# Two-layer encoder trunk in float32: nine pairs of column blocks a layer take seven block products instead of eight in their first two K chunks

## The chip, the cores and the metric

The kernel runs on one core of a Trainium2 chip, in one launch. The metric is the device time of that execution in microseconds (us), as the median of several runs. TensorE (PE) multiplies, VectorE (DVE) and ScalarE (ACT) work elementwise, GpSimd (POOL) does a few small powers, and the queue of SyncE (SP) issues all the transfers. Each engine works through its own instructions in the order of the program.

## The reference

A trunk of 2 layers on 256 tokens of width 2048, all in float32. Cut to what matters:

```python
for l in range(DEPTH):                              # 2
    h = rmsnorm(x, pre_norm_g[l])
    proj = jnp.einsum('bsd,dn->bsn', h, w_in[l])    # 2048 x 17920: 35 column blocks of 512
    (qa, ka, va, qb, kb, vb, qc, kc, vc, za, zb, zc, gates) = jnp.split(proj, split_points, axis=-1)
    ya = neighbourhood_attention(qa, ka, va, rpb[l])            # 8 heads
    yb = gqa_attention(rope(rmsnorm(qb)), rope(rmsnorm(kb)), vb)  # 8 heads
    yc = dilated_mixture(qc, kc, vc)                            # 12 heads in 3 groups
    ga, gb, gc = jnp.split(sigmoid(gates + b_gate[l]), 3, axis=-1)
    merged = (ga * ((ya * silu(za)) @ w_branch_a[l]) + gb * ((yb * silu(zb)) @ w_branch_b[l])
              + gc * ((yc * silu(zc)) @ w_branch_c[l]))
    out = jnp.einsum('bsd,de->bse', merged, w_out[l])           # 4 column blocks of 512
    x = x + rmsnorm(out, post_norm_g[l])
```

## The kernel before, in words

**A product in three matmuls.** Every float32 operand is split in two halves of type fp32r, high and low (`split`, and `emit_hi` / `emit_lo` for weights): a cast on ACT gives the high half, a subtraction on DVE the low one. `mm3` (L169) multiplies high by high, high by low and low by high into the same accumulator, and leaves out low by low. So one block product (128 of K, 128 tokens, 512 columns) is three matmuls of 128x128 by 128x512.

**Blocks, chunks, halves.** The work is a list of column blocks (`Blk`) of 512 columns: first the projections of the dilated mixer C (one gate block, three of q, three of k, three of v), then those of A (two units of four blocks), then B (five), then four merges (`merge`: three gate blocks, then three branch projections of 8, 4 and 8 K tiles, in the order a, c, b), then four output blocks. A block's K is cut into chunks of 256, that is one transfer of 512 KB (`raw`), one cast (`wh`) and one subtraction (`wl`) of 128x1024. The tokens are two halves T of 128, each with an accumulator (`acc`) of its own. `stream` is the list of all chunks; for each chunk `run_half` issues six matmuls for T = 0 and six for T = 1. In the last block of a layer and the first of the next (`lag`) the second half runs six chunks behind the first.

**How far ahead things are written.** The program writes the instructions of all engines in one loop over (chunk, half). Ahead of each half `ahead` writes the transfers up to 6 chunks, casts up to 3 and subtractions up to 2 chunks ahead of the one that is multiplied (more in `far` blocks). What is written first on an engine is done first there. All tiles of weights and most others come from one pool `up` of 47 tiles of 4 KB a partition; accumulators come from the pool `mm` of 4 banks, with four more banks for scores (`sc`), head outputs (`o`) and transposes (`tp`, two).

**What runs in between.** After the second half of a chunk there is a slot (`slot`, L102). In it the kernel takes two steps of waiting evacuations (`evq`: one of a half block, as a rule), a step of each active job, and starts a job: light ones are the turns of a finished block (`tr_job`: DVE transposes of 32x32, a transfer to DRAM and back, then a split), heavy ones the heads of attention. So the evacuation of a block's first half is written in the slot after its last chunk, that of its second half one slot later. `hold` keeps all evacuations of a layer back until the sum of squares of x is there (`stats`, written after chunk 5 of the second block, `second`).

**The pair that there is already.** The first two output blocks (`mate`, `mated`) are interleaved: six chunks of the one, six of the other, then the last two of each, since the last merged block arrives late.

**Where the change touches.** The list `order` of (chunk, half) is made at the end, before the main loop (L756 to L772). The change makes it where the stream is made.

## Time and profile before

| | us or share |
|---|---|
| median of 3 runs | 2019.52 (2019.33 to 2019.94) |
| profiled execution, its own time | 2019.99 |
| profiled execution, its span | 2017.9 |
| TensorE's share of the chain of waits that ended last | 92% |

The span is from the first to the last instruction of the profiled execution; its own time has some 2.1 us around it. In the groups of instructions an operation is named by its line, engine and tiles, with how many there are, their busy time and the mean of one in ns. Matmuls are pipelined, so the duration of one overlaps with the next; how fast they follow one another is read from their starts. An idle time stands with what ended it: "<-DVE wl L202" is a wait for the subtraction of line 202. HBM was read at 231 GB/s over the span.

### The profile page before, as it was taken

To read this page: it belongs to the slowest core of one execution; us is meant where nothing else is said; L and a number is where in the kernel's file an instruction comes from. 1 tells how busy PE (TensorE), PEld (TensorE's weight loads), DVE (VectorE), ACT (ScalarE), POOL (GpSimd) and SP (SyncE) were. 2 spreads that over 40 slices of the span, in tenths; PEclk is the share of its full clock that TensorE was granted. 3 is DMA by queue.
4 is the path that set the end of the run, shared out by engine and by line. 5 is a ranking of instruction groups with operands and counts; after the bars stand their busy time and mean duration, and the time that the engine had idled before them with its cause. 6 is when DMAs were issued, how large, how long until landed. Compare 5 with 4: busy or idle time off the path is not lost.

```text
span 2017.9 us, 24528 instructions
## 1 busy us (share of the span) xinstructions
PE 2002.0 (99%) x9098; PEld 1660.7 (82%) x9098; DVE 1271.1 (63%) x1565; ACT 995.9 (49%) x1482; POOL 21.5 (1%) x31
## 2 busy tenths in 40 slices
PE   9999999999999999999999999999999999999998
PEld 7888888888788888888888888888887888888886
DVE  6554576768677465645665545767677775646554
ACT  6544465646464444443564444555465644443432
POOL 0000000000000000000000000000000000000000
PEclk9999999999999999999999999999999999999999
DMA  8667467756666756675647664768566666556653
GB/s 330 245 258 269 158 248 258 262 209 239 226 245 236 267 189 227 225 239 213 235 166 266 263 243 146 266 234 301 198 246 234 239 243 246 214 198 233 219 220 124
DMA packets 171720, 468.06 MB, mean 232 GB/s; under 512 B 15440, under 2 KB 58576, under 8 KB 171600
## 3 DMA queue, kind: packets, MB, share of 16 engines
q1 hardware_dynamic: 171600, 466.50, 63.9%
q8 instruction: 71, 1.16, 0.2%
q14 instruction: 49, 0.40, 0.1%
HBM read 427.11 MB, written 39.32 MB: 231 GB/s over the span
## 4 chain that ended last, share of the span: by engine, by line
PE 92%; DVE 3%; ACT 3%; DMA 1%; issue 0%; SPq 0%; DVEq 0%; POOLq 0%; ACTq 0%
PE acc L173 30%; PE acc L174 30%; PE acc L172 30%; ACT wh L197 1%; DVE wl L202 1%; DVE tt L150 1%; ACT sp L373 1%; PE o L174 0%; PE o L173 0%; PE o L172 0%; ACT sp L384 0%; DMA raw<-in_wpack_dram 0%; PE sc L174 0%; PE sc L450 0%; PE o L480 0%
## 5 line engine op out<-in xcount | busy, mean ns | idle before, releaser
L202 DVE TENSOR_TENSOR wl<-raw,wh 128x1024 fp32r<-128x1024 f32 (+1 forms) x706 | 833.7, 1214 | 169.9 <-ACT wh L197 169.7
L173 PE MATMUL acc<-wl,hTh 128*128 128x512 f32 x2240 | 873.6, 390 | 5.1 <-DVE wl L202 5.1
L172 PE MATMUL acc<-wh,hTh 128*128 128x512 f32 x2240 | 875.6, 391 | 0.6 <-ACT wh L197 0.6
L174 PE MATMUL acc<-wh,hTl 128*128 128x512 f32 x2240 | 872.0, 389 | 0.0
L197 ACT CAST wh<-raw 128x1024 fp32r<-128x1024 f32 (+1 forms) x706 | 706.2, 1042 | 268.4 <-DMA raw<-in_wpack_dram 155.3
L173 PEld LDWEIGHTS acc<-wl,hTh 128*128 128x128 f32 x2240 | 420.9, 188 | 94.8 <-DVE wl L202 10.0
L174 PEld LDWEIGHTS acc<-wh,hTl 128*128 128x128 f32 x2240 | 420.5, 188 | 87.7
L172 PEld LDWEIGHTS acc<-wh,hTh 128*128 128x128 f32 x2240 | 420.9, 188 | 87.0 <-ACT wh L197 1.8
L172 PE MATMUL acc<-wh,yTh 128*128 128x512 f32 x320 | 124.5, 389 | 0.0
L173 PE MATMUL acc<-wl,yTh 128*128 128x512 f32 x320 | 124.5, 389 | 0.0
L174 PE MATMUL acc<-wh,yTl 128*128 128x512 f32 x320 | 124.5, 389 | 0.0
L598 ACT ACTIVATE g<-g 128x512 f32<-128x512 f32 x48 | 30.4, 633 | 177.7 <-DVE g L597 177.7
L597 DVE SCALAR_TENSOR_TENSOR g<-acc,rsx,bg 128x512 f32<-128x512 f32 x48 | 35.9, 747 | 127.9 <-PE acc L174 127.8
L172 PE MATMUL acc<-wh,mTh 128*128 128x512 f32 x256 | 100.0, 390 | 0.0
L174 PE MATMUL acc<-wh,mTl 128*128 128x512 f32 x256 | 99.6, 389 | 0.0
L173 PE MATMUL acc<-wl,mTh 128*128 128x512 f32 x256 | 99.6, 389 | 0.0
L373 ACT ACTIVATE sp<-sp,nm 128x256 f32<-128x256 f32 (+1 forms) x48 | 27.6, 577 | 131.4 <-DVE nm L368 131.4
L150 DVE STREAM_TRANSPOSE tt<-tok 128x512 f32<-128x512 f32 (+1 forms) x72 | 73.3, 1057 | 0.0
L609 DVE SCALAR_TENSOR_TENSOR g<-g,acc 128x512 f32<-128x512 f32 x48 | 32.8, 684 | 61.2 <-PE acc L174 61.1
L174 PEld LDWEIGHTS acc<-wh,yTl 128*128 128x128 f32 x320 | 60.1, 188 | 12.5
L172 PEld LDWEIGHTS acc<-wh,yTh 128*128 128x128 f32 x320 | 60.1, 188 | 12.3
L173 PEld LDWEIGHTS acc<-wl,yTh 128*128 128x128 f32 x320 | 60.1, 188 | 12.3
(111 smaller groups left out, 1086.5 us busy)
## 6 DMA issues: line engine op xcount, KB each, us to landing
raw<-in_wpack_dram SPq DMA_DIRECT2D x558, 512.0 KB, 6.5
raw<-in_wo_dram SPq DMA_DIRECT2D x64, 512.0 KB, 7.6
turn<-tt SPq DMA_DIRECT2D x50, 512.0 KB, 3.0
tx<-turn SPq DMA_DIRECT2D x50, 512.0 KB, 5.6
raw<-in_wa_dram SPq DMA_DIRECT2D x32, 512.0 KB, 3.4
raw<-in_wb_dram SPq DMA_DIRECT2D x32, 512.0 KB, 4.6
turn<-tt SPq DMA_DIRECT2D x34, 256.0 KB, 2.2
tx<-turn SPq DMA_DIRECT2D x34, 256.0 KB, 4.3
```

Source lines behind the costliest of these rows:

```text
L150: nc.vector.transpose(out=tt[:, :, T].rearrange("p j (h a) -> p h j a", h=n), in_=srcs[T].rearrange("p (h b j) -> p h j b", h=n, j=4))
L172: nc.tensor.matmul(out_, lhsT=lh, rhs=rh, start=first, stop=False)
L173: nc.tensor.matmul(out_, lhsT=lh, rhs=rl, start=False, stop=False)
L174: nc.tensor.matmul(out_, lhsT=ll, rhs=rh, start=False, stop=last)
L197: nc.scalar.copy(HI[i][:, k], RAW[i][:, k])
L202: nc.vector.tensor_tensor(out=LO[i][:, k], in0=RAW[i][:, k], in1=f32(HI[i][:, k]), op=ALU.subtract)
L373: nc.scalar.activation(p[:, i], sc[:, i], AF.Exp, bias=nm[:, i:i + 1], scale=1.0 if f is None else f[:, i:i + 1], accum_out=sm[:, i:i + 1])
L597: nc.vector.scalar_tensor_tensor(g, ps, S["rs"][T], BG[i], op0=ALU.mult, op1=ALU.add)
L598: nc.scalar.activation(g, g, AF.Tanh, scale=0.5)
L609: nc.vector.scalar_tensor_tensor(G[i][:, T], G[i][:, T], 1.0, ps, op0=ALU.add, op1=ALU.mult)
```

## The change

In a pair of blocks that stand next to each other the first two chunks are taken together. For a chunk of 256 of K, two blocks of 512 columns and 256 tokens, the activations are a 2x2 matrix of blocks (token half by K tile) and the weights one (K tile by column block); their product takes eight block products, and seven by Strassen's method in Winograd's form. The pairs are the eight blocks of mixer C after the first two (four pairs), the first two gate blocks of each merge (four pairs) and the first two output blocks.

- Four combinations of the activations (`combos`) are made for each of the first two chunks of a layer's h and of its merged rows, five DVE operations and a split each. They are written behind the first half of chunks 6 and 7 of the block `second`, and of chunks 1 and 2 of the last merge's last branch projection.
- For each unit (one chunk of both blocks) DVE makes four combinations of the weights in two tiles (`unit_hi`), in the order of the program ahead of the cast of B. A is the first block's chunk as it is, B and C are combinations, D is one of them and is taken for both units in one tile.
- The seven products of both units are summed into seven accumulators, at most six at a time, in the steps s1 to s6 of `two_blocks`; the plain chunk 2 of the two blocks is put between them. Four sums on DVE (`total`) and a copy on ACT bring the products together in two tiles (`keep`), and `whole` adds one of these to each accumulator, in place, ahead of its evacuation.
- Ahead of and in a pair (`near`: from three chunks before it) transfers run 8, casts 6 and subtractions 5 places ahead, at most two of each for one half.
- The pool `mm` has six banks, and transposes take the tags of `sc` and `o`.
- From chunk 3 the chunks of the two blocks alternate; the interleaving of the first two output blocks by sixes is gone.

```diff
+LA_UNIT, NEAR = 5, 4
+UNITS = 2
...
-    mm = ctx.enter_context(tc.tile_pool(name="mm", bufs=4, space=PSUM))
+    mm = ctx.enter_context(tc.tile_pool(name="mm", bufs=6, space=PSUM))
...
-        tp = aux.tile([P, 4, P], F32, name="tp", bufs=2)
+        flow["tp"] += 1
+        tp = aux.tile([P, 4, P], F32, name="tp", tag=("sc", "o")[flow["tp"] % 2])
...
+    def unit_hi(u, what):
+        if what == "B":
+            r1, r2 = RAW[u, "A"], RAW[u, "B"]
+            ta, tb = U("ta", [2, 512]), U("tb", [2, 512])
+            minus(ta[:, 0], r2[:, 0], r1[:, 0])
+            minus(ta[:, 1], r2[:, 1], ta[:, 0])
+            minus(tb[:, 0], r2[:, 1], r2[:, 0])
+            minus(tb[:, 1], r1[:, 1], ta[:, 1])
+            RAW[u, "D"] = RAW.pop((u, "B"))
+            RAW[u, "B"], RAW[u, "C"] = ta, tb
+        if what == "D":
+            u.h["D"] = U("wh", [2, 512], FR)
+            for k, v in enumerate(u.all):
+                nc.scalar.copy(u.h["D"][:, k], RAW[v, "D"][:, 1])
+        else:
+            u.h[what] = U("wh", [2, 512], FR)
+            nc.scalar.copy(u.h[what], RAW[u, what])
...
     def ahead(i):
         n = len(stream)
         b = stream[i][0]
         la, room = (8, 13) if b.far else (0, 6)
+        near = any(isinstance(x[0], Unit) for x in stream[i:i + NEAR])
+        if near:
+            la, room = LA_UNIT, 12
...
-            most = 9 if key == "raw" else flow["split"]
+            most = 9 if key == "raw" else min(flow["split"], 2) if near else flow["split"]
...
+    def product(ps_, units, lhs, what, k, alone):
+        for n, u in enumerate(units):
+            x = units[0] if what == "D" else u
+            h, lo = x.h[what], x.lo[what]
+            q = n if what == "D" else k
+            mm3(ps_, lhs(u), (h[:, q], lo[:, q]), n == 0, alone and n == len(units) - 1)
+
+    def two_blocks(one, two):
...
+        for u in units:
+            stream.extend([(u, "A"), (u, "B")])
+        p1 = len(stream)
+        stream.append((one, UNITS))
+        stream.extend((u, "C") for u in units)
+        d = len(stream)
+        stream.append((head, "D"))
+        rest = len(stream)
+        stream.append((two, UNITS))
+        for kc in range(UNITS + 1, one.nc):
+            stream.extend([(one, kc), (two, kc)])
...
+        def s1():
+            new("p1", "p5")
+            product(bank["p1"], units, plain(0, 0), "A", 0, True)
+            product(bank["p5"], units, comb(0), "B", 0, True)
+            keep["c11"], keep["p16"] = room()
+            nc.scalar.copy(keep["c11"], bank.pop("p1"))
+        def s2():
+            new("a")
+            product(bank["a"], units, plain(1, 0), "A", 1, False)
+        def s3():
+            new("p6")
+            product(bank["p6"], units, comb(1), "B", 1, True)
+            total("p16", bank.pop("p6"), keep["c11"])
...
+        def s4():
+            new("d")
+            product(bank["d"], units, plain(1, 1), "C", 1, False)
+            keep["c12"], keep["c21"] = room()
+            total("c12", bank.pop("p5"), keep["p16"])
+        def s5():
+            new("p7")
+            product(bank["p7"], units, comb(2), "C", 0, True)
...
+        def s6():
+            new("c")
+            product(bank["c"], units, comb(3), "D", 0, False)
...
+            total("c21", bank["p7"], keep["p16"])
+            keep["c22"] = keep.pop("p16")
+            total("c22", bank.pop("p7"), keep["c12"])
+            new("w")
+        def whole(evac, of):
+            def f(T, x):
+                k = keep.pop(of[T])
+                nc.vector.tensor_tensor(out=x, in0=x, in1=k, op=ALU.add)
+                yield from evac(T, x)
+            return f
...
+        order.extend([(p1 - 1, s1), (p1, s2), (p1, 0), (p1, s3), (d - 1, s4), (p1, 1), (d, s5), (d, s6),
+                      (rest, 0), (rest + 1, 0), (rest, 1), (rest + 1, 1)])
+        order.extend((i, T) for i in range(rest + 2, len(stream)) for T in range(2))
...
+        def combos(stat, kc):
+            h, lo, j = stat(2 * kc)
+            t = U("cf", [2, 512])
+            a = t[:, 0].rearrange("p (k n) -> p k n", k=2)
+            c = t[:, 1].rearrange("p (k n) -> p k n", k=4)
+            nc.vector.tensor_tensor(out=a, in0=f32(h[:, j:j + 2]), in1=f32(lo[:, j:j + 2]), op=ALU.add)
+            a11, a21, a12, a22 = (a[:, k, T * P:(T + 1) * P] for k in range(2) for T in range(2))
+            nc.vector.tensor_tensor(out=c[:, 0], in0=a21, in1=a22, op=ALU.add)
+            minus(c[:, 1], c[:, 0], a11)
+            minus(c[:, 2], a11, a21)
+            minus(c[:, 3], a12, c[:, 1])
+            r = U("cs", [2, 4, P], FR)
+            split(c, r[:, 0], r[:, 1])
+            return r
...
+            gs = [proj(23 + 4 * i + nb, evac_g(i), pre=pre(i)) for i in range(3)]
+            gs[0].pair(gs[1])
...
+        for k in (1, 3, 5, 7):
+            cb[k].pair(cb[k + 1])
+        for kc in range(UNITS):
+            second.at("after", (6 + kc, 0), lambda kc=kc: CH.update({kc: combos(stat_h, kc)}))
...
-        outs[0].mate, outs[1].mated = outs[1], True
+        outs[0].pair(outs[1])
+        for kc in range(UNITS):
+            blocks[-5].at("after", (1 + kc, 0), lambda kc=kc: CM.update({kc: combos(stat_m, kc)}))
...
     for i, T in order:
         b, kc = stream[i]
+        if callable(T):
+            ahead(i)
+            T()
+            if T.__name__ in ("s1", "s3", "s5"):
+                slot()
+            continue
```

## Rows read from the trace of the kernel before

**Rows 1.** The page: busy time of each engine, its share, its instructions.

```profile
PE 2002.0 (99%) x9098; PEld 1660.7 (82%) x9098; DVE 1271.1 (63%) x1565; ACT 995.9 (49%) x1482; POOL 21.5 (1%) x31
```

**Rows 2.** Groups of instructions: line, engine, operation, count, busy us, mean ns, idle before.

```profile
L172 PE MATMUL acc<-wh,hTh 128*128 128x512 f32 x2240 | 875.6, 391 | 0.6 <-ACT wh L197 0.6
L202 DVE TENSOR_TENSOR wl<-raw,wh 128x1024 fp32r<-128x1024 f32 x702 | 831.1, 1217 | 169.8 <-ACT wh L197 169.7
L197 ACT CAST wh<-raw 128x1024 fp32r<-128x1024 f32 x702 | 703.9, 1045 | 268.4 <-DMA raw<-in_wpack_dram 155.3 <-DMA raw<-in_wo_dram 44.3 <-PE acc L173 23.7
...
L611 DVE TENSOR_TENSOR g<-g 128x512 f32<-128x512 f32 x32 | 22.1, 691 | 1.1
...
L132 ACT ACTIVATE qkh<-tx 128x512 fp32r<-128x512 f32 x32 | 18.4, 623 | 10.6 <-DMA tx<-turn 10.6
...
L525 DVE TENSOR_TENSOR s<-acc,ropeg 128x128 f32<-128x128 f32 x8 | 1.9, 283 | 0.0
```

**Rows 3.** Waits: who waited for whom, us in total, times, longest.

```profile
PE acc L173 <- DVE wl L202: 5.1, 9, 1.2
```

**Rows 4.** Timeline of TensorE, end of layer 0's last merge: start us, us, instruction.

```profile
916.70 0.39 PE L172 MATMUL acc<-wh,yTh 128*128 128x512 f32 x1
...
919.42 0.39 PE L172 MATMUL acc<-wh,mTh 128*128 128x512 f32 x1
```

**Rows 5.** Timeline of DVE there, idle time before in brackets.

```profile
910.56 0.69 DVE L611 TENSOR_TENSOR g<-g 128x512 f32<-128x512 f32 x1
911.17 3.49 DVE L202 TENSOR_TENSOR wl<-raw,wh 128x1024 fp32r<-128x1024 f32 x3
918.26 0.69 DVE L609 SCALAR_TENSOR_TENSOR g<-g,acc 128x512 f32<-128x512 f32 x1 [3.60 <-PE acc L174]
...
923.18 2.04 DVE L150 STREAM_TRANSPOSE tt<-g 128x512 f32<-128x512 f32 x2
...
934.05 1.29 DVE L134 TENSOR_TENSOR mTl<-tx,mTh 128x512 fp32r<-128x512 f32 x2 [4.32 <-ACT mTh L132]
```

**Rows 6.** Timelines of DVE and ACT, second block of layer 0.

```profile
39.46 1.23 DVE L202 TENSOR_TENSOR wl<-raw,wh 128x1024 fp32r<-128x1024 f32 x1 [1.09 <-ACT wh L197]
...
43.16 0.16 DVE L249 TENSOR_REDUCE v<-ss 128x2 f32<-128x8 f32 x1 [0.15 <-ACT junk L245]
...
44.63 0.15 DVE L256 SCALAR_TENSOR_TENSOR rsx<-rs_y 128x2 f32<-128x2 f32 x1
...
51.04 0.69 ACT L330 ACTIVATE tok<-acc,rsx 128x512 f32<-128x512 f32 x1 [3.07 <-PE acc L174]
```

**Rows 7.** Timelines of DVE and ACT, second block of layer 1.

```profile
1025.08 8.03 DVE L202 TENSOR_TENSOR wl<-raw,wh 128x1024 fp32r<-128x1024 f32 x7
...
1054.04 0.69 ACT L330 ACTIVATE tok<-acc,rsx 128x512 f32<-128x512 f32 x1 [12.22 <-PE acc L174]
```

**Rows 8.** Busy time by stretch, mixer C: us, PE, PEld, DVE, ACT, POOL.

```profile
56.00:99.00 43.00, 43.00 (x191) 35.59 (x191) 23.30 (x22) 20.81 (x27) 0.00 (x0) 1.00 0.70 260
```

**Rows 9.** Busy time of layer 0's first merge, first two blocks; DVE's timeline before.

```profile
540.00:583.50 43.50, 41.68 (x201) 34.26 (x200) 34.19 (x60) 25.85 (x52) 1.01 (x1) 1.00 0.63 218
...
530.57 1.16 DVE L150 STREAM_TRANSPOSE tt<-sp 128x256 f32<-128x256 f32 x2
```

**Rows 10.** Timeline of DVE, end of layer 0's first merge.

```profile
726.21 3.49 DVE L202 TENSOR_TENSOR wl<-raw,wh 128x1024 fp32r<-128x1024 f32 x3
733.30 0.69 DVE L609 SCALAR_TENSOR_TENSOR g<-g,acc 128x512 f32<-128x512 f32 x1 [3.60 <-PE acc L174]
```

**Rows 11.** TensorE at start and end; the column after POOL is its clock.

```profile
1.45 4.45 PE L89 MATMUL acc<-warm 128*128 128x512 bf16 x10 [1.45 <-DVE warm L86]
...
2009.21 0.39 PE L174 MATMUL acc<-wh,mTl 128*128 128x512 f32 x1
...
2012.00:2014.00 2.00, 0.00 (x0) 0.00 (x0) 2.00 (x4) 0.00 (x0) 0.00 (x0) 0.95 0.55 200
2014.00:2016.00 2.00, 0.00 (x0) 0.00 (x0) 0.05 (x1) 0.00 (x0) 0.00 (x0) 0.50 0.98 308
```

More of the change, by code (lines that the diff above doesn't have):

```diff
@@ L39, in __init__, with pair @@
         self.far = False
-        self.mate = None
-        self.mated = False
+        self.twin = None
+        self.twinned = False
         self.before = {}
         self.after = {}
+    def pair(self, other):
+        self.twin, other.twinned = other, True
     def at(self, when, key, f):
         getattr(self, when).setdefault(key, []).append(f)
+class Unit:
+    far = False
+    def __init__(self, one, two, kc):
+        self.one, self.two, self.kc = one, two, kc
+        self.h, self.lo = {}, {}
 @with_exitstack
@@ L92, in trunk @@
     evq, light, heavy, active = deque(), deque(), deque(), []
-    flow = dict(turn=0, cool=0, hold=True, slot=0, split=9)
+    flow = dict(turn=0, tp=0, cool=0, hold=True, slot=0, split=9)
     def later(g, wait=0):
@@ L179, in trunk @@
     RAW, HI, LO = {}, {}, {}
+    order, ps = [], {}
     def emit_raw(i):
         b, kc = stream[i]
+        if isinstance(b, Unit):
+            if kc in "AB":
+                x = (b.one, b.two)[kc == "B"]
+                if b.kc == 0 and x.pre:
+                    x.pre()
+                RAW[b, kc] = U("raw", [2, 512])
+                nc.sync.dma_start(out=RAW[b, kc], in_=x.w[b.kc].rearrange("p (k n) -> p k n", k=2))
+            return
         if kc == 0 and b.pre:
@@ L203, in emit_lo, with minus, unit_lo @@
         del RAW[i]
+    def minus(out_, a, b):
+        nc.vector.tensor_tensor(out=out_, in0=a, in1=b, op=ALU.subtract)
+    def unit_hi(u, what):
[15 more added lines that the diff above has]
+            nc.scalar.copy(u.h[what], RAW[u, what])
+    def unit_lo(u, what):
+        u.lo[what] = U("wl", [2, 512], FR)
+        if what == "D":
+            for k, v in enumerate(u.all):
+                minus(u.lo["D"][:, k], RAW[v, "D"][:, 1], f32(u.h["D"][:, k]))
+                del RAW[v, "D"]
+        else:
+            minus(u.lo[what], RAW[u, what], f32(u.h[what]))
+            del RAW[u, what]
     def ahead(i):
@@ L219, in run_half @@
         b, kc = stream[i]
+        first = 2 * UNITS if b.twinned and T else -1 if b.twin or b.twinned else 0
         wh, wl = HI[i], LO[i]
@@ L615, in evac_p @@
                 return f
-            for i in range(3):
-                proj(23 + 4 * i + nb, evac_g(i), pre=pre(i))
+            gs = [proj(23 + 4 * i + nb, evac_g(i), pre=pre(i)) for i in range(3)]
+            gs[0].pair(gs[1])
             for i, w, nk, ub in ((0, wbr_a, 8, (("a", 0), ("a", 1))), (2, wbr_c, 4, (("c", 0),)),
@@ L723, in trunk @@
         for b in bl:
-            if b.mate:
-                m = b.mate
-                stream += [(b, kc) for kc in range(6)] + [(m, kc) for kc in range(6)]
-                stream += [(c, kc) for c in (b, m) for kc in range(6, 8)]
-            elif not b.mated:
-                stream += [(b, kc) for kc in range(b.nc)]
+            i = len(stream)
+            if b.twin:
+                two_blocks(b, b.twin)
+            elif not b.twinned:
+                stream += [(b, kc) for kc in range(b.nc)]
+                if b.lag:
+                    a = [(i + k, 0) for k in range(b.nc)]
+                    c = [(i + k, 1) for k in range(b.nc)]
+                    order += a[:LAG]
+                    for k in range(b.nc - LAG):
+                        order += [a[LAG + k], c[k]]
+                    order += c[b.nc - LAG:]
+                else:
+                    order += [(i + k, T) for k in range(b.nc) for T in range(2)]
     nc.sync.dma_start(out=gpre, in_=pre_g)
@@ L754, in trunk @@
     st["hi"] = st["lo"] = 7
-    order = []
-    i = 0
-    while i < len(stream):
-        b = stream[i][0]
-        n = b.nc
-        if b.lag:
-            a = [(i + k, 0) for k in range(n)]
-            c = [(i + k, 1) for k in range(n)]
-            order += a[:LAG]
-            for k in range(n - LAG):
-                order += [a[LAG + k], c[k]]
-            order += c[n - LAG:]
-        else:
-            n = 1
-            order += [(i, T) for T in range(2)]
-        i += n
-    ps = {}
     for i, T in order:
         b, kc = stream[i]
+        if callable(T):
[4 more added lines that the diff above has]
+            continue
         for f in b.before.get((kc, T), ()):
```

59 lines of the change are left out of this document (50 added, 9 removed).

## The prediction, made before the change was run

> **What bounds the kernel now.** I read the page first. TensorE is busy 99% of the span, VectorE (DVE) is busy 63%, ScalarE (ACT) 49% [rows 1]. Then the groups of instructions: 2240 × 3 of the matmuls are of one form, and the reader is to see next to them the splitting of the weights, a cast on ACT (1.05 us) and a subtraction on DVE (1.22 us) for each chunk [rows 2]. TensorE waits in all 5.1 us for that subtraction [rows 3]. So time falls only with the number of matmuls, as long as DVE delivers in time. The timeline gives the price of a matmul: a chunk of twelve begins at 916.70 and the next at 919.42, so 2.72 us a chunk and 0.227 us a matmul [rows 4] (the 0.39 us of the groups overlaps with the next matmul).
>
> **What it removes.** A pair's first two chunks were 8 block products of 6 matmuls each; seven are left. That is 6 matmuls a pair, 18 pairs in two layers, 108 × 0.227 = **24.5 us**.
>
> **What it adds on DVE and ACT.** Per pair, by the groups [rows 2]: eight differences of 128x512 (0.69 each [rows 2]; 0.61 from one to the next that doesn't need it, 910.56 to 911.17 [rows 5], so 2.6 for the four of a unit), 5.2 us; seven chunks to split instead of four (two each of A, B and C, and two halves of D), 3 × 1.16 = 3.5 us with the spacing of 3.49 for three [rows 5]; four sums and four additions ahead of the evacuations, 8 × 0.69 = 5.5 us. Together 14 us of DVE a pair, 18 × 14 = 252 us, so DVE goes to some 76%. ACT gets 3 casts and a copy, 3.8 us a pair. Four times (two chunks, two stages) a layer the combinations of the activations come on top: one 0.69, four of 128x128 at 0.28, a cast of 0.62 on ACT that DVE waits for, a subtraction of 0.69, with two hand-overs 3.2 us (2.5 to 4). In-place additions in PSUM are shown by no row; the nearest reads PSUM and writes SBUF in 0.69 (918.26 [rows 5]), I take 0.69, at most a second pass over, 1.4, which the range carries.
>
> On the share alone all this hides. But DVE works through its instructions in the order in which they are written, and the pair's work is written only from three chunks (8.2 us) ahead of its first product, behind the evacuation before it. So each entry into a pair is a sum: from when DVE can begin, to when the product needs it. The first product needs A of the second unit 0.7 us after the pair's start, the second product needs B and the combination of the second unit 2.0 us after it (six matmuls and three).
>
> *Output pair, one a layer.* DVE has the last evacuation behind it at 911.17 and the pair would begin at 919.42 [rows 4, 5]; in between DVE now does three subtractions and is idle from 914.7 to 918.3, where it waits for TensorE [rows 5]. After: the last chunk's subtraction 1.16, four differences 2.6, A 1.16, a combination 3.2, four differences 2.6, B, A and B 3.5, the other combination 3.2. That is 17.4, so 928.6 where 921.5 is needed: TensorE is **7.1 us** late (5.5 with the combinations at 2.5, 10 if the next sums hold up an accumulator as well). Two of them: 14.2.
>
> *First pair of layer 0.* DVE ends a subtraction at 40.7, and the block before the pair ends its first half at 51.04, so the pair would begin at 52.4 and need the combination at 54.4 [rows 6]. DVE's list from 40.7: differences 2.6, two subtractions 2.3, the statistics 1.6 (43.16 to 44.8, most of it a wait for GpSimd), differences 2.6, two subtractions 2.3, an evacuation that was held back 0.7, one subtraction 1.16, a combination 3.2, an evacuation 0.7, a subtraction 1.16, the second combination 3.2: 21.5, so 62.2. **7.8 us** late (5 to 10). It can't begin sooner: each subtraction there waits for its cast, 1.09 us at 39.46, as ACT squares x in between.
>
> *First pair of layer 1.* The same list, but DVE is through with its subtractions at 1033.1 and the half ends at 1054.04 [rows 7]; the list ends near 1053.6, the need is at 1057.4. Nothing (0 to 2).
>
> *The other three pairs of that stage, six in all.* DVE is busy 23.3 of 43.0 us [rows 8]; with 14.3 more it is 37.6 of the 42.2 that a pair takes. It fits, with the next pair's differences done in the idle middle. The accumulator of the second block's second half is free 0.3 us before the seventh product wants it; I take 0.5 us a pair, **3** (0 to 12).
>
> *Pair of the first merge, one a layer.* Here heads of attention run beside it: DVE is busy 34.2 of 43.5, and TensorE already loses 1.8 of the 43.5 [rows 9]. From 531.7 (a transpose ends) [rows 9] DVE would do a subtraction, differences, a subtraction, differences and two subtractions, 9.8 us, so A of the second unit is there at 541.5 where it is needed near 538.3. Then a head's maximum 0.85, two subtractions and a norm 2.6, the evacuation of the block before (about 2.4, and waits for ACT's squares of some 2), C twice 2.3: about 551.7 where the fifth product wants it at 545.8. That is 5.9, and the evacuation of the second half, cut into steps of later slots, holds an accumulator for 0 to 6 us more; 1.8 of it is lost today too. I take 5 each, **10** (−3 to 22).
>
> *Merges 2 to 4, six in all.* Begin 726.2, pair at 734.7 (the first half ends at 733.3) [rows 10]; no combination here, so 9.8 us to the second unit's A: 736.0 against 735.4. 0.7 us, and with the two evacuations, the transposes of the merge before and four chunks in the queue the sum that frees an accumulator comes up to 2.3 us late. I take 1.2, **7** (2 to 18).
>
> Everything else is unchanged or hidden: the casts on ACT (the pool has two accumulators more, and the transposes' two tiles move to tags that no head uses at the layer's turn), the transfers (the same weights are read; a turn waits on SP for DVE's transposes; the one that the output pair's last chunks need takes 10.9 us from its transposes to the split [rows 5], which would begin near 939 and so be split near 951, and is used first near 958).
>
> **Sum.** −24.5 + 7.8 + 14.2 + 3 + 10 + 7 = **+17.5 us**. The profiled execution took 2019.99 (span 2017.9 and 2.1 around it), so 2037.5; its own time is 0.5 above the median of 2019.52, so **2037**.
>
> [...]
>
> **Rivals.**
> *The lead is enough.* The lists above are too long because DVE overlaps and begins earlier than I reckon. Place: the pairs' entries. For it: DVE is idle 37% of the time [rows 1], ACT 12.2 us in one piece before layer 1's first pair [rows 7], and TensorE's waits are only 5.1 us in all. Against it: these idle pieces lie in front of evacuations, behind which the order holds the new work. Price: the full 24.5 us comes through but for the 0.7 at the merges' entries: 2019.5 − 24.5 + 5 = 2000 (1995 to 2012). It decides where a list ends before the second product: 7 us shorter at the output pair, 8 at layer 0.
> *Only the combinations are late.* The two long entries stand, all other pairs run free: −24.5 + 7.8 + 14.2 = −2.5, so 2017 (2012 to 2024).
> *Buffers bind too.* The pool of 47 holds the weights' tiles, and by the code a pair holds some 25 of them at its fourth step (eight pairs of halves, combinations, sums and four transfers ahead) against 10 of an ordinary stretch; transfers and casts then wait for products, 1.5 us or more in each of 18 pairs: 2037 + 27 = 2064 (2050 to 2090). For it: today casts already wait for TensorE to free a tile, 23.7 us on one line [rows 2]; against: the tiles that are freed by the second and fourth product come before the need.
>
> **How the numbers follow.** Forecast 0.47 (its own range 2024 to 2050), the lead is enough 0.30, only the combinations 0.12, buffers 0.11. The range takes in most of the second and ends above the forecast's bounds: 1998 to 2056; outside are about 0.06 below and 0.09 above. 0.2% is 4 us, what can be told from no change here: faster is the first rival and half of the next, 0.35; the same 0.06; slower 0.59.
>
> **What would show it.** Matmul instructions 108 fewer (each with its weight load). TensorE idle at five places, released by DVE: 6 to 8 us in the pair near 52, about 7 in both output pairs, some 5 in the first merges; the releaser at the output pairs is the combination's subtraction, not the weights'. No wait at 1055. If TensorE keeps 0.227 us through the entries, the lists are wrong and the time is near 2000; if waits stand in all eighteen pairs, it is the buffers. DVE's busy time should rise by about 270 us; if by much more, the additions in PSUM are dearer than 0.69.

## The result and the profile after

The changed kernel took 2068.19 us (median of 4 runs, 2066.40 to 2070.55) against 2019.73 before (2019.33 to 2020.50): ratio 1.024 [1.0222, 1.0258], slower by 48.5 us. The direction was forecast, the size was not: +17.5 was said, and the time lies above the range. The profiled run took 2070.55.

The matmuls went as they should, 108 fewer than in [rows 1]. VectorE (DVE) got 258.7 us more work; 270 was forecast. The page's line of busy times:

```profile
PE 2006.3 (97%) x8990; PEld 1652.1 (80%) x8990; DVE 1529.8 (74%) x1973; ACT 1066.4 (52%) x1580; POOL 21.5 (1%) x31
```

The groups that answer to [rows 2] (count | busy us, mean ns of one | idle before). The additions in place in PSUM (L397) and the sums (L345) take the 0.69 us that was assumed:

```profile
L397 DVE TENSOR_TENSOR acc<-acc,keep 128x512 f32<-128x512 f32 x72 | 49.8, 692 | 74.9 <-PE acc L190 74.9
L345 DVE TENSOR_TENSOR keep<-acc,keep 128x512 f32<-128x512 f32 x72 | 49.3, 684 | 0.6
```

ScalarE's casts wait for TensorE to free tiles 28.4 us in all, against 44.0 before (us in total, times, longest; the first three lines are of the changed kernel). So the pool holds them up no more than it did:

```profile
ACT wh L225 <- PE acc L189: 17.2, 16, 2.2
ACT wh L257 <- PE acc L189: 9.1, 3, 3.1
ACT wh L225 <- PE acc L190: 2.1, 2, 1.7
...
ACT wh L197 <- PE acc L173: 23.7, 10, 4.2
ACT wh L197 <- PE acc L174: 20.3, 15, 3.9
```

The waits of TensorE, against the 5.1 us of [rows 3] (us in total, times, longest). L237 is a subtraction in a pair, L233 one elsewhere, L147 the combinations' cast, L345 a sum that frees an accumulator, L721 rope:

```profile
PE acc L189 <- DVE wl L237: 17.9, 13, 3.5
PE acc L189 <- DVE wl L233: 12.6, 13, 3.3
PE acc L188 <- ACT cs L147: 10.4, 4, 3.3
PE acc L188 <- DVE keep L345: 7.2, 4, 2.6
PE acc L188 <- DVE s L721: 2.7, 2, 1.4
```

These are 50.8 us. What is lost besides the waits is seen where one of them ends. Layer 0's first pair, by stretches of 2 us (us, then the busy time of PE, PEld, DVE, ACT and POOL, then TensorE's granted clock). Before, the stretches of [rows 8, 9] have 1.00:

```profile
54.00:56.00 2.00, 0.00 (x0) 0.00 (x0) 1.43 (x5) 0.41 (x1) 0.00 (x0) 1.00 0.00 0
56.00:58.00 2.00, 1.52 (x3) 0.58 (x3) 1.75 (x3) 1.73 (x3) 0.00 (x0) 0.65 0.00 0
58.00:60.00 2.00, 0.00 (x0) 0.00 (x0) 1.93 (x5) 0.00 (x0) 0.00 (x0) 0.50 0.00 0
60.00:62.00 2.00, 0.89 (x2) 0.67 (x3) 1.24 (x4) 1.57 (x3) 0.00 (x0) 0.50 0.00 0
62.00:64.00 2.00, 2.00 (x6) 1.62 (x6) 2.00 (x3) 2.00 (x5) 0.00 (x0) 0.50 0.04 8
64.00:66.00 2.00, 2.00 (x7) 1.54 (x6) 2.00 (x3) 2.00 (x4) 0.00 (x0) 0.50 0.00 0
66.00:68.00 2.00, 2.00 (x9) 1.60 (x7) 2.00 (x4) 2.00 (x3) 0.00 (x0) 0.79 0.55 215
```

TensorE idles for 3.06 and 3.32 us with three matmuls between, and the granted clock goes from 1.00 to 0.50. Then there are six or seven matmuls in 2 us instead of ten or eleven. The same at the output pair, in TensorE's timeline (start us, us; the wait in brackets): 0.43 us from one start to the next, 0.227 from 954.46 on.

```profile
945.77 0.50 PE L189 MATMUL acc<-wl,mTh 128*128 128x512 f32 x1 [3.53 <-DVE wl L237]
...
949.28 0.79 PE L188 MATMUL acc<-wh,cs 128*128 128x512 f32 x1 [2.08 <-ACT cs L147]
...
953.28 0.63 PE L188 MATMUL acc<-wh,mTh 128*128 128x512 f32 x1
953.71 0.63 PE L189 MATMUL acc<-wl,mTh 128*128 128x512 f32 x1
...
954.46 0.39 PE L188 MATMUL acc<-wh,mTh 128*128 128x512 f32 x1
954.68 0.39 PE L189 MATMUL acc<-wl,mTh 128*128 128x512 f32 x1
```

**A tally for every run.** For each matmul I take the time from its start to the start of the next; what this exceeds 0.227 us by counts as lost (matmuls of fewer columns are given less than 0.227). Summed over the run, 21.5 us are lost before and 95.5 after, 74.0 more; less 24.5 for the 108 matmuls this gives +49.5, and the profiled runs differ by 50.6. By place, both layers together, what was lost more than before, and how much of it went while matmuls followed one another in 0.43 us:

| place | forecast | after | of it at 0.43 us a matmul |
|---|---|---|---|
| layer 0's first pair | 7.8 | 10.1 | 2.8 |
| two output pairs | 14.2 | 16.7 | 4.8 |
| other pairs of C | 3 | 8.4 | 3.2 |
| pair of the first merge, two | 10 | 13.5 | 4.7 |
| entries of merges 2 to 4, six | 7 | 12.7 | 3.5 |
| third gate blocks of the first merge, two | not listed | 7.3 | 1.6 |
| plain chunks in the pairs of merges 3 and 4 | not listed | 4.0 | 0 |
| sum | 42 | 72.7 | 20.6 |

The two places that were not listed have different causes. In the first merge's third gate block (614 and 1636) VectorE does the four additions and the evacuations of the pair beside a change of heads. In the pairs of merges 3 and 4 (874, 1806 and 1899) TensorE waits 0.9 to 1.2 us, some 26 us behind the pair's start. There VectorE stands still for the turn of the merge before, and the subtractions that TensorE needs are written behind it:

```profile
873.50 1.29 DVE L149 TENSOR_TENSOR mTl<-tx,mTh 128x512 fp32r<-128x512 f32 x2 [5.67 <-ACT mTh L147]
...
875.99 0.50 PE L189 MATMUL acc<-wl,hTh 128*128 128x512 f32 x1 [1.17 <-DVE wl L233]
```

The kernel before has this wait of VectorE too (7.16 us at 844.41), and TensorE does not wait there. The expectations of experiments 6 and 8 count these waits of merges 3 and 4 to the third gate blocks; by the timelines they stand inside the pairs.

### The profile page after: what moved, and what is told of

It is laid out like the page before. It is cut to its first block, busy times and chain, and to the rows that moved or that the text cites. A ratio compares the mean times of both kernels' runs of the same rounds, so it can differ in the third digit from the quotient of the medians.

```text
span 2068.2 us, 24958 instructions
## 1 busy us (share of the span) xinstructions
PE 2006.3 (97%) x8990; PEld 1652.1 (80%) x8990; DVE 1529.8 (74%) x1973; ACT 1066.4 (52%) x1580; POOL 21.5 (1%) x31
## 4 chain that ended last, share of the span: by engine, by line
PE 75%; DVE 13%; DMA 5%; ACT 3%; issue 3%; SPq 0%; DVEq 0%; POOL 0%; ACTq 0%; POOLq 0%
PE acc L189 24%; PE acc L188 24%; PE acc L190 24%; DVE wl L233 3%; DMA raw<-in_wpack_dram 2%; DVE wl L237 2%; DVE tt L166 1%; DMA tx<-turn 1%; DVE ta L237 1%; DVE tb L237 1%; DMA turn<-tt 1%; ACT wh L225 1%; DMA x<-in_x_dram 1%; DVE acc L397 0%; DVE keep L345 0%
## 5 line engine op out<-in xcount | busy, mean ns | idle before, releaser
L189 PE MATMUL acc<-wl,hTh 128*128 128x512 f32 x2080 | 816.5, 393 | 22.4 <-DVE wl L233 11.5
L188 PE MATMUL acc<-wh,hTh 128*128 128x512 f32 x2080 | 817.4, 393 | 3.0 <-DVE s L721 2.7
L190 PE MATMUL acc<-wh,hTl 128*128 128x512 f32 x2080 | 813.7, 391 | 0.0
L233 DVE TENSOR_TENSOR wl<-raw,wh 128x1024 fp32r<-128x1024 f32 (+1 forms) x634 | 751.3, 1212 | 65.3 <-ACT wh L225 63.9
L225 ACT CAST wh<-raw 128x1024 fp32r<-128x1024 f32 (+1 forms) x634 | 633.6, 1041 | 171.8 <-DMA raw<-in_wpack_dram 98.8
L189 PEld LDWEIGHTS acc<-wl,hTh 128*128 128x128 f32 x2080 | 393.2, 189 | 111.4 <-DVE wl L233 16.9
L188 PEld LDWEIGHTS acc<-wh,hTh 128*128 128x128 f32 x2080 | 393.2, 189 | 85.3 <-issue 3.5
L397 DVE TENSOR_TENSOR acc<-acc,keep 128x512 f32<-128x512 f32 x72 | 49.8, 692 | 74.9 <-PE acc L190 74.9
L257 ACT CAST wh<-ta 128x1024 fp32r<-128x1024 f32 x36 | 37.9, 1053 | 120.3 <-DVE ta L237 117.5
L188 PE MATMUL acc<-wh,cs 128*128 128x512 f32 x144 | 59.9, 416 | 17.6 <-ACT cs L147 10.4
L189 PEld LDWEIGHTS acc<-wl,yTh 128*128 128x128 f32 x320 | 60.1, 188 | 14.2 <-DVE wl L233 2.0
```

Of the source, the lines that this page charges most:

```text
L188: nc.tensor.matmul(out_, lhsT=lh, rhs=rh, start=first, stop=False)
L189: nc.tensor.matmul(out_, lhsT=lh, rhs=rl, start=False, stop=False)
L190: nc.tensor.matmul(out_, lhsT=ll, rhs=rh, start=False, stop=last)
L225: nc.scalar.copy(HI[i][:, k], RAW[i][:, k])
L233: nc.vector.tensor_tensor(out=LO[i][:, k], in0=RAW[i][:, k], in1=f32(HI[i][:, k]), op=ALU.subtract)
L257: nc.scalar.copy(u.h[what], RAW[u, what])
```

## The experiments

Theory 1: VectorE works in written order (in the changed kernel the cast of 867.34 is done at 868.39, and its subtraction runs at 874.71, behind the turn's two of 873.50). Its list at an entry into a pair (what it has to do between the last instruction that can't move and the first use) takes longer than the lead that the program gives it, so TensorE idles, and the clock falls behind the idle time (from 1.00 to 0.50 in the stretches from 56 on). Rival: tiles and accumulators hold the work back.

**1. Combinations earlier.**

```diff
-            second.at("after", (6 + kc, 0), lambda kc=kc: CH.update({kc: combos(stat_h, kc)}))
+            blk, key = (second, (6 + kc, 0)) if l else (first, (2 + 2 * kc, 0))
+            blk.at("after", key, lambda kc=kc: CH.update({kc: combos(stat_h, kc)}))
...
-            blocks[-5].at("after", (1 + kc, 0), lambda kc=kc: CM.update({kc: combos(stat_m, kc)}))
+            blocks[-8].at("after", (4 + 2 * kc, 0), lambda kc=kc: CM.update({kc: combos(stat_m, kc)}))
```

> The changed kernel with one edit: the combinations of the activations are written earlier. Those of layer 0's h stand behind chunks 2 and 4 of the first block (before: behind chunks 6 and 7 of the second), those of the merged rows behind chunks 4 and 6 of the last merge's third gate block (before: in the last branch projection; layer 1's h is left where it was). Theory 1 (VectorE works in the written order, its list at a pair's entry is longer than the lead, TensorE idles, and its granted clock falls after the idle time): layer 0's first pair loses 0 to 2 us instead of 10.1 and keeps the clock at 1.00; each output pair loses 0 to 2 instead of 8.5 and 8.2; in all 2068 - 24 = 2044 us (2040 to 2050), if the third gate block bears the extra VectorE work. Rival (tiles of the pool and accumulators hold the work back, not the lists): the same waits stand with another releaser, 2064 to 2072.

2048.95 us (1.0144 [1.0127, 1.0161]). The waits for ACT cs L147 are gone from the view of waits:

```profile
PE acc L189 <- DVE wl L233: 15.2, 15, 3.3
PE acc L189 <- DVE wl L237: 11.9, 13, 2.2
PE acc L188 <- DVE keep L345: 7.7, 5, 2.1
```

Layer 0's first pair lost 0 (10.1 after), the entries of the output pairs 0.7 each (8.5 and 8.2); layer 0's lost 0.9 more further in, where VectorE waits for the last merge's turn. But 4.0 us were lost at 27 to 34, in the first block, where the combinations stand now: 6.2 us in one piece on VectorE (22.12 to 28.27), a wait of 2.2 and a fall of the clock. So 2049 and not 2044. The same accumulators and tiles with another place in the list: the list is the cause at these three entries.

**2. TensorE kept busy in the waits.**

```diff
+    def busy(n):
+        t = aux.tile([P, 512], F32, name="fill", tag="sc")
+        for _ in range(n):
+            nc.tensor.matmul(t, lhsT=warm[:, 0, 0:P], rhs=warm[:, 1], start=True, stop=True)
...
-            product(bank["p5"], units, comb(0), "B", 0, True)
+            product(bank["p5"], units, comb(0), "B", 0, True, one.fill)
...
+        outs[0].fill = 8
+        if l == 0:
+            cb[1].fill = 13
```

> The changed kernel with dummy matmuls (bf16, 128x512, into a scores bank that nobody reads then) put where TensorE idles at an entry: 13 ahead of each unit's second product in layer 0's first pair, 8 ahead of each unit's in both output pairs. They compute nothing that is used. They take 2.9 and 1.8 us each time at full clock, less than the waits they stand in (3.1 and 3.3; 3.5 and 2.1), so if nothing else happens the time stays 2068. Theory 1 says that the idle time there is followed by a fall of the granted clock to 0.50, which costs 2.7 us at layer 0's first pair and 2.2 at each output pair on top of the waits: the clock stays near 1.00 in 58 to 66 and in 948 to 954, and the time falls by 5 to 7 us, to about 2062. Rival (the slow matmuls there come from something else, such as accumulators or weight loads beside VectorE's writes): the slow stretches stay and the time is 2068 or more.

2066.69 us (1.0230 [1.0214, 1.0245]). The clock behaved as theory 1 says; stretches of this kernel to set beside those above:

```profile
56.00:58.00 2.00, 1.91 (x7) 0.89 (x8) 1.93 (x3) 1.55 (x3) 0.00 (x0) 1.00 0.00 0
58.00:60.00 2.00, 2.00 (x10) 0.78 (x8) 1.93 (x6) 0.00 (x0) 0.00 (x0) 1.00 0.00 0
60.00:62.00 2.00, 1.22 (x5) 0.61 (x5) 1.24 (x3) 1.76 (x3) 0.00 (x0) 1.00 0.00 0
62.00:64.00 2.00, 2.00 (x10) 1.65 (x9) 2.00 (x3) 2.00 (x5) 0.00 (x0) 1.00 0.00 0
```

It stayed at 1.00 there and at layer 0's output pair, with ten matmuls in 62 to 64 instead of six. The saving was missed: 1.5 us, not 5 to 7. At the output pairs I had put the dummies one product too late, behind the first wait of 3.53, so they lengthened what they should fill; in layer 1 the clock still fell (mean of the profiled run 0.991; 0.987 in the changed kernel, 0.999 before). At layer 0's first pair 26 dummies (5.9 us) and 2.1 lost, 8.0 together, stand against 10.1.

**3. Waits put into the kernel before.**

```diff
     def emit_lo(i, ks=(slice(0, 2),)):
+        for _ in range(stream[i][0].idle if stream[i][1] == 6 else 0):
+            nc.vector.tensor_tensor(out=idle_t, in0=idle_t, in1=idle_t, op=ALU.add)
```

> The kernel before with extra additions on VectorE (128x256, some 0.4 us each, whose result nobody uses) ahead of the subtraction of chunk 6 in three blocks of mixer C in each layer: 16, 21 and 28 of them in layer 0, 18, 24 and 34 in layer 1. A block's subtractions are written two chunks ahead, so TensorE should wait at six places for about 1 to 10 us. Theory 1: short waits cost their own length and the clock stays at 1.00; from some length on the granted clock in the stretch behind the wait is 0.50 and the twelve or so matmuls there cost 0.43 us instead of 0.227, some 2 us more than the wait, once for each wait however long. Rival (a wait costs only its length; the slow matmuls of the changed kernel belong to the pairs): no slow stretch behind any of the six. The time should be 2020 plus the waits, some 25 to 40, plus 2 for each wait that lets the clock fall.

2034.64 us, one run. VectorE had more room than I reckoned: three of the six places show no wait, the others 3.23, 1.37 and 5.99 us. Stretches around the first, behind the second, around the third:

```profile
157.00:159.00 2.00, 0.18 (x1) 0.19 (x2) 1.97 (x4) 0.00 (x0) 0.00 (x0) 0.86 0.07 27
159.00:161.00 2.00, 2.00 (x5) 1.62 (x6) 2.00 (x3) 0.00 (x0) 0.00 (x0) 0.50 0.00 0
...
1122.00:1124.00 2.00, 2.00 (x9) 1.66 (x10) 2.00 (x2) 0.00 (x0) 0.00 (x0) 1.00 0.02 8
...
1169.00:1171.00 2.00, 0.00 (x0) 0.00 (x0) 1.90 (x5) 0.00 (x0) 0.00 (x0) 0.50 0.00 0
1171.00:1173.00 2.00, 1.23 (x3) 1.04 (x4) 2.00 (x3) 0.00 (x0) 0.00 (x0) 0.50 0.01 4
1173.00:1175.00 2.00, 2.00 (x6) 1.52 (x6) 2.00 (x2) 0.00 (x0) 0.00 (x0) 0.50 0.00 0
```

Without any pair the plain waits of 3.23 and 5.99 us were followed by a clock of 0.50 and cost 1.5 and 1.9 us more; that of 1.37 was followed by 1.00 and cost itself. The rival on the clock falls: slow matmuls do not need a pair. The length of the wait does not decide alone: a wait of 3.3 us in the first merge's third gate block was followed by 1.00 in the changed kernel (3.31 us, up to 618.16) and by slow matmuls in experiment 1 (607), and there one of 2.2 us (27) was followed by slow ones too.

**4. Differences on GpSimd.**

```diff
-            minus(ta[:, 0], r2[:, 0], r1[:, 0])
...
+            def gminus(o, x, y):
+                nc.gpsimd.tensor_tensor(out=o, in0=x, in1=y, op=ALU.subtract)
+            gminus(ta[:, 0], r2[:, 0], r1[:, 0])
```

> The changed kernel with the four differences of the weights of each unit (128x512, 36 units) on GpSimd instead of VectorE. VectorE's lists get 5.2 us shorter for each pair. No row shows GpSimd on this shape; from its multiplications of 128x256 in the rotary tables (0.87 us) I estimate 1.7 us each, 7 us a unit, and it reads and writes SBUF beside VectorE. Theory 1, if GpSimd keeps up: the merges' entries lose 0 to 3 us instead of 5 to 9, the output pairs 3 to 5 instead of 8, layer 0's first pair 5 to 7 instead of 10, in all 2040 (2030 to 2055). If GpSimd's 14 us a pair are themselves the late list, the waits stand with GpSimd as releaser and it is 2065 to 2100. Rival (tiles and accumulators): no change, 2064 to 2072.

2098.83 us (1.0388 [1.0373, 1.0404]), the slower branch of the expectation. Groups of GpSimd, and of ScalarE's cast that waits for it:

```profile
L245 POOL TENSOR_TENSOR tb<-raw,ta 128x512 f32<-128x512 f32 x36 | 78.6, 2183 | 0.0
L245 POOL TENSOR_TENSOR ta<-raw 128x512 f32<-128x512 f32 x36 | 73.7, 2046 | 957.5 <-DMA raw<-in_wpack_dram 265.1 <-PE acc L190 244.5 <-DVE wl L233 189.9
...
L259 ACT CAST wh<-ta 128x1024 fp32r<-128x1024 f32 x36 | 37.8, 1051 | 122.4 <-POOL ta L245 122.4
```

The four groups make 7.5 us a unit against 2.6 on VectorE, so ScalarE stands still for GpSimd and TensorE behind it. It shows nothing on the rival.

**5. Six pairs, and 6. twelve.** `for k in (1, 3, 5)` in C and no other pair; then with `if nb in (2, 3)` in the merges and the output pair besides.

> The changed kernel with six of its eighteen pairs: the first three of mixer C in each layer. The fourth of C, the four of the merges and that of the output blocks are taken as in the kernel before (the output blocks interleaved by sixes again). Layer 0's combinations of h stand behind chunk 4 of the first block and chunk 2 of the second. Six accumulators and the rest stay. Theory 1 (a pair is worth the 1.36 us of its six matmuls wherever its list fits into the lead): these six pairs lost nothing in the runs so far, so 2020 - 6 x 1.36 = 2012 (2010 to 2015), with layer 0's first pair and the block before it free of waits. Rival (the change costs something everywhere, by accumulators, shared tags of the transposes or VectorE's share): 2018 or more.

> The changed kernel with twelve of its eighteen pairs: the first three of mixer C, those of the third and fourth merge and that of the output blocks, in each layer; the combinations are written early (layer 0's h behind chunk 4 of the first block and chunk 2 of the second, the merged rows' behind chunks 4 and 6 of the last merge's third gate block). Theory 1: -12 x 1.36 = -16.3 us, and what the merges 3 and 4 and the output pair lost with early combinations, 0.7 at each entry and 0.7 to 1.4 in the third gate block, 9.3 in both layers: 2020 - 7 = 2013 (2010 to 2017), the like of six pairs. Rival (the pairs left out are not what cost): 2030 or more.

2016.73 (0.9983 [0.9975, 0.9992]) and 2016.93 (0.9986 [0.9977, 0.9995]): both faster than before by a sixth of a per cent, both by less than expected; the first lies between the theory's range (to 2015) and the rival's (from 2018). The tally accounts for it: six pairs, −8.2 and 5.0 more lost than before; twelve, −16.3 and 14.3. In both, 4 us go at 78 to 84, behind layer 0's first pair. ScalarE's timeline of the first shows why:

```profile
71.57 1.05 ACT L227 CAST wh<-raw 128x1024 fp32r<-128x1024 f32 x1 [6.09 <-DMA raw<-in_wpack_dram]
74.55 1.15 ACT L515 COPY z<-tx 128x512 f32<-128x512 f32 x2 [1.93 <-DMA tx<-turn]
77.41 1.15 ACT L149 ACTIVATE qkh<-tx 128x512 fp32r<-128x512 f32 x2 [1.72 <-DMA tx<-turn]
```

It waits for transfers: weights, then two turns whose DVE transposes the pair had made late (57.99 and 64.08), and the casts stand behind the turns. That the weights' own transfers queued behind the turns on SP is how I read the idle DMA at 55 to 60 (its share in the changed kernel is 0.00 there, the column behind the clock in the stretches above); it was not tried alone. One cast there (64.43) also waited 4.02 us for TensorE to free a tile.

**7. A longer lead.** `LA_UNIT, NEAR = 8, 7`.

> All eighteen pairs, the combinations early (layer 0's h behind chunk 4 of the first block and chunk 2 of the second, the merged rows' as before), and the lead ahead of a pair made longer: casts 9 and subtractions 8 places ahead instead of 6 and 5, from six places before the pair instead of three. With the old lead I reckon 2045. Theory 1 (the lists are longer than the lead): the entry of the first merge loses 3 to 5 us instead of 9.4, of the second 0 to 1 instead of 4.9, of the others 0 instead of 0.7; the last pair of C and the third gate block keep their waits: 2030 (2022 to 2040). Rival (tiles and accumulators limit): nothing gained, 2043 to 2060, casts wait for TensorE to free tiles.

2045.45 us (1.0125 [1.0111, 1.0139]). The 2045 for the old lead was reckoned, not run; experiment 1, with layer 0's combinations at another place, took 2049. So little or nothing was gained in the sum, as the rival said. Its sign came too: the casts' waits for tiles grew from 28 us in the changed kernel to 87. But experiment 9 has 74 us of them at the same lead and loses only 4.7 more than the kernel before, so I do not take them for the cause. Merges 3 and 4 and the output pairs lost nothing now, C's last pair 0.9 (2.4 and 3.7 in experiment 1). Layer 0's first pair lost 6.5: TensorE waits 3.65 us for an evacuation (L554 at 57.71) that is now written behind the pair's differences. The first two merges lost more than in experiment 1 (22 us against 20 in layer 0), at a new place. TensorE and DVE at the end of the first merge's last branch projection:

```profile
654.26 0.80 PE L188 MATMUL acc<-wh,yTh 128*128 128x512 f32 x1 [7.24 <-ACT yTh L147]
```

```profile
649.05 1.22 DVE L237 TENSOR_TENSOR wl<-raw,wh 128x1024 fp32r<-128x1024 f32 x1
650.18 1.22 DVE L237 TENSOR_TENSOR wl<-ta,wh 128x1024 fp32r<-128x1024 f32 x1
...
652.64 0.42 DVE L584 TENSOR_TENSOR z<-o,z 128x256 f32<-128x256 f32 x1
```

The next pair's list was now written ahead of the last head's gate (L584), on which this projection waits: 7.24 us here, 6.60 in layer 1. At merges 3 and 4 and the output pairs the longer lead removed the wait; at the first merges, where attention still runs, it only changed which work was late.

**8. The two blocks one after the other.** In the pairs of C and the merges chunks 3 to 7 of the first block ahead of those of the second: `stream.extend((b, kc) for b in (one, two) for kc in ks)`.

> All eighteen pairs, the combinations early as in the run with the longer lead, the lead as in the changed kernel; in the pairs of C and of the merges chunks 3 to 7 of the first block are done before those of the second, instead of in turns, so that the first block's two evacuations come eleven microseconds before the second's. With turns I reckon 2045. Theory 1a (the waits in the merges' third gate blocks and in C's last pair come from four evacuations written at one place, 0.69 + 0.75 us each on VectorE): the 3.3 us waits near 614 and 1636 and those of 0.7 to 1.4 in merges 3 and 4 go, and the 2.3 in C's last pair: 2028 (2020 to 2036). Rival (they come from the heads of attention beside them, or from the entry itself): the waits stay, 2042 to 2050.

2045.47 us (1.0118 [1.0102, 1.0133]; single runs from 2041 to 2051). The waits of 3.3 and 3.1 in the first merges' third gate blocks fell to 2.2, those in merges 3 and 4 stayed, and in C two new ones a layer, of 1.3 to 1.8 us, replaced the one in the last pair. Theory 1a fails as put; for merges 3 and 4 it could not hold, as their waits come from the turn.

**9. Thirteen pairs.** `((3, 5, 7), (1, 3, 5, 7))[l]` in C, `nb in (2, 3)`, the output pair, the longer lead of experiment 7, the merged rows' combinations early.

> Thirteen pairs, those that the runs so far show with little loss at the longer lead (casts 9 and subtractions 8 places ahead, from six places before a pair): mixer C but for layer 0's first, the third and fourth merge, the output pair; the merged rows' combinations behind chunks 4 and 6 of the last merge's third gate block. Without layer 0's first pair its list and the transfers behind it go, without the first two merges the heads of attention run as before. Theory: -13 x 1.36 = -17.7 us, 0.9 lost in each layer's last pair of C, the rest free: 2020 - 16 = 2004 (2001 to 2010), faster than both kernels. Rival (VectorE's additional work costs by its sum, wherever it stands): 12 pairs at the shorter lead gave 2017, so 2015 or more.

2006.77 us (0.9934 [0.9921, 0.9946]), the only clear gain on both kernels. Waits of TensorE:

```profile
PE acc L189 <- DVE wl L233: 6.1, 11, 1.2
...
PE acc L188 <- DVE keep L345: 1.3, 2, 0.7
```

VectorE is busy 1463 us, 192 more than before, and TensorE loses only 4.7 more: −17.7 + 4.7 = −13.0, measured −13.2. So it is not VectorE's sum that costs.

**10. The second merge's pair without the first's.** `nb in (1,)`, C's second and third pair (in layer 1 the first too), no other.

> Of the eighteen pairs seven: mixer C's second and third in layer 0, first to third in layer 1, and the second merge's in both, at the lead of the changed kernel; output blocks as in the kernel before. The question is why the second merge's entry lost 4.9 us and not the 1.2 forecast. Theory 2a (the first merge's pair makes the last head of attention late, and its tail then stands in the second merge's entry): with the first merge unpaired the entry loses 0.7 like those of merges 3 and 4, and 2020 - 7 x 1.36 + 2 x 1 = 2012.5 (2011 to 2014.5). Theory 2b (the heads' tail stands there anyway, and the entry's own list is too long): it loses 4.9 again, 2020 - 9.5 + 9.8 = 2020 (2018 to 2021).

2019.56 us (0.9999 [0.9990, 1.0008]): 2b. The entry lost 3.1 and 4.7. DVE's timeline there has no idle time from the last head's y to the pair:

```profile
627.23 1.23 DVE L151 TENSOR_TENSOR yTl<-z,yTh 128x1024 fp32r<-128x1024 f32 x1 [1.13 <-ACT yTh L149]
...
632.68 0.69 DVE L809 TENSOR_TENSOR g<-g 128x512 f32<-128x512 f32 x1
633.29 0.69 DVE L239 TENSOR_TENSOR ta<-raw 128x512 f32<-128x512 f32 x1
...
642.89 1.22 DVE L239 TENSOR_TENSOR wl<-ta,wh 128x1024 fp32r<-128x1024 f32 x1
```

The differences begin only behind the branch projections' evacuations, and the second unit's A ends at 642.98, when TensorE has waited 2.23 us for it.

**11. The first merge without its differences.** In `unit_hi`, for that pair, `RAW[u, "C"] = r1` and B as it came.

> All eighteen pairs with the combinations early (layer 0's h behind chunk 4 of the first block and chunk 2 of the second), but in the first merge's pair of each layer the four differences of the weights a unit are left out (the products there take the plain weights, so the result of this stage is not the reference's): 5.2 us less on VectorE in one pair of each layer, the same matmuls, casts and accumulators. With them this form should take 2045. Theory (VectorE's list at the entry of the first merge, beside the heads, is what costs 9.4 us there): the loss between the pair's start and its end falls by 5 us or more, to 2 to 4, and a little of the 3.3 to 5 in the third gate block goes too: 2045 - 11 = 2034 (2030 to 2038). Rival (accumulators, or the heads' own order): the loss there stays at 8 or more, 2042 to 2046.

2038.51 us (1.0094 [1.0079, 1.0109]). The loss there fell from 9.4 and 8.9 (experiment 1) to 6.7 and 5.5: between the two expectations. What stands is a wait of 3.2 for a sum (L353 in this kernel), so there the list of differences is a third of the price, and that this sum stands among the heads' work is how I read most of the rest. The kernel before lost 2.1 us a layer in this stretch too.

**12. The first merge without its additions.** `whole` leaves out the addition in that pair.

> The kernel with early combinations (2049, waits of 3.3 and 3.1 us in the first merge's third gate block), but in the first merge's pair of each layer the four in-place additions ahead of the evacuations are left out (the accumulators then lack what the products kept aside, so that stage is not the reference's): 4 x 0.69 = 2.8 us less on VectorE at the place before those waits, everything else the same. Theory (it is the sum of VectorE's list from the pair's end to there): the waits fall by 2.8 to 0.3 to 0.7, the clock stays up behind them, 2049 - 2 x 2.8 - 1.7 = 2042 (2040 to 2045). Rival (only what stands between the last two subtractions counts: one addition, one evacuation, the last head's gate, VectorE's wait for ScalarE's cast of y, y's low half and the next head's start, 7.2 us from one to the next): the waits fall by 0.7 only, to 2.4 to 2.6, and it is 2047 (2045 to 2049).

2037.77 us (1.0083 [1.0066, 1.0100]). The waits fell from 3.3 and 3.1 to 0.9 and 0.7, by 2.4 of the 2.8 us taken away: the theory, not the rival. The time fell further than expected, 11 us; the tally of the profiled runs gives 7.7, with falls of the clock gone at 607 and 1209. The second is luck: it stands in layer 1's mixer C, which the edit does not touch. TensorE's waits in layer 0, experiment 1 first:

```profile
610.31 0.50 PE L189 MATMUL acc<-wl,hTh 128*128 128x512 f32 x1 [3.32 <-DVE wl L233]
...
608.95 0.50 PE L190 MATMUL acc<-wl,hTh 128*128 128x512 f32 x1 [0.93 <-DVE wl L234]
```

## Why the size was wrong

The tally gives +49.5 where +17.5 was said. Of these 32 us the clock is 20.6, the places that were not listed are 9.7 without the clock, and 1.7 is the rest.

- **Right.** The 24.5 us (every profiled run's tally balances within 1.1 us with 0.227 a matmul), VectorE's additional work, 0.69 for the additions, no wait at layer 1's first pair, 0.7 at the entries of merges 3 and 4. At the output pairs the signs were half right: the longer wait (3.53) ends with a subtraction of the weights, and only the second with the combination. The output pair's list was reckoned 17.4 us long; from the first difference at 932.92 to the second combination's end at 949.95 it is 17.0. Taken together the listed places lost 42.4 us without the clock; 42 was forecast. That the sum agrees so closely is luck: terms that were too small (C, merges 2 to 4) and too large (output pairs, first merges) cancel.
- **Failed: every wait was priced at its own length.** The sum has no term for slow matmuls behind a wait. In the changed kernel the granted clock went to 0.50 behind waits at ten places, and 6 to 13 matmuls followed one another in 0.43 us instead of 0.227 at each: some 2 us a place, 20.6 us in all. With three matmuls between two waits the clock went from 1.00 to 0.50 (56 to 60), and behind one wait alone it did too (5.99 us, experiment 3). Experiments 2 and 3 show it from both sides: 1.00 with dummies in the waits, 0.50 behind waits put into the kernel before.
- **Failed: what stands in and behind a pair was not listed.** "Everything else is unchanged or hidden" passed over two places, 9.7 us without the clock. In the first merge's third gate block, where four additions and four evacuations meet a head's change, it is 5.7; experiment 12 shows the additions to be most of the wait, experiment 8 that spreading the blocks' ends is not enough. In the pairs of merges 3 and 4 it is 4.0, from the turn that VectorE waits for; this is read from the timelines. With the longer lead these waits are gone (experiment 7).
- **Failed: "Merges 2 to 4, six in all".** The entry at 734.7 [rows 10], called there the end of the first merge, is that of the second; so I read the third merge's entry and took the second's for the like of it. It lost 4.9, and experiment 10 shows that the first merge's pair is not needed for that.
- **Mis-sized: "the other three pairs of that stage".** 3 forecast, 8.4 lost, all in the last pair of each layer: TensorE waits 2.3 and 2.6 us for the sum that frees an accumulator (L345 at 201.23 in layer 0), and 3.2 are the clock behind it. Ahead of this sum VectorE waits 0.82 us for ScalarE's half of v and does two transposes (2.10); which of them makes it late was not tried.
- **The rivals.** "The lead is enough" fell with the waits, "only the combinations are late" with experiment 1, where 29 us stay with them early, and "buffers bind too" with the casts' waits, which fell from 44.0 to 28.4 us, and experiments 1 and 9. Its 2064 was near the result by luck, as the mechanism was another.

What stays open: why the first merge's pair loses 6 us without its differences (the kernel before lost 2.1 there); why the clock falls behind one wait and not behind another of the same length; and whether the transfers behind layer 0's first pair are held by SP's queue.

## What to carry to other kernels

A saving on the engine that bounds is worth what the feeding engine's list allows at each entry: write that list out from the last instruction that can't move to the first use, and for what stands behind the change as well. Price an idle time of the matmul engine with the slow stretch that the trace shows behind it (here some 2 us at each of ten places). Before one gives a change up, let it go only to the places whose lists fit: thirteen of eighteen places at the longer lead gained 13 us, where all eighteen at that lead lost 25 (48 as the change was made).

## What the runs showed of the hardware

- Behind waits inside the kernel the granted clock went from 1.00 to 0.50, and some ten matmuls took 0.43 us instead of 0.227; not behind each of them (1.00 behind 1.37 us in experiment 3 and behind 3.31 us in the changed kernel). Four runs of experiment 8 lie between 2041 and 2051, with mean clocks of 0.992 to 0.995, where the kernel before took 2019 to 2022 in all its runs (0.998 to 0.999); other kernels with such waits spread by 2 to 5 us.
- GpSimd took 1.6 to 2.2 us for a 128x512 difference that takes VectorE 0.69, and in that run two of VectorE's subtractions in the pairs took 1529 (`wl<-ta`) and 1907 ns (`wl<-raw`) instead of 1218.
- An addition of 128x512 in place in PSUM took 692 ns, one that reads PSUM and writes SBUF 684.
